# Two layers of a hybrid trunk: the down projection as plain sums over all channel tiles in place of a Strassen form

## The chip, the cores and the metric

The kernel runs on one core of one Trainium2 chip. The metric is the device time of one execution in microseconds (us).

## The reference

Two layers work on 1024 latent and 128 context tokens of 1024 channels, in float32. Each layer has a mixer (retention, Fourier mixing, latent attention, long convolution) and then a channel sub-layer. The change lies in the end of the channel sub-layer, the product with `w_down`, and in what comes right after it:

```
h = rmsnorm(x, norm[2]) * (1.0 + sc2) + sh2
f = (jax.nn.silu(h @ p['w_gate']) * (h @ p['w_up'])) @ p['w_down']
x = x + g2 * rmsnorm(f, norm[3])
```

`w_down` is 2816 x 1024 per layer. The next layer begins with `rmsnorm(x, norm[0]) * (1.0 + sc1) + sh1` and the input projection.

## The kernel before

The 1152 tokens are nine tiles of 128 (tile 8 is the context, `CTX`), the 2816 hidden channels are 22 tiles (`NF`). A float32 product is made of three products of split operands: `split` (L119 to L125) writes a rounded high part on ACT (L120) and the remainder on DVE (L125), and `mm3` (L127 to L131) issues three matmuls, high by high, high by low and low by high, each with 128 hidden channels and 128 tokens as the stationary operand and 512 columns moving. PSUM holds a 128x512 float32 block in a bank.

`channels(l)` runs `phase3` and `gate_up`, which writes the hidden rows tile by tile to DRAM (`self.hd`), and then `ffn(l)` (L1469 to L1705):

- The down projection is Winograd's form of Strassen's product over pairs of token tiles (0,1), (2,3), (4,5), (6,7), halves of a chunk of hidden channels and halves of the 1024 columns. `DOWN` names four chunks. For each chunk and pair, seven products (`product`, L1599) take the place of eight; tile 8 goes alone with four products.
- `load_w`, `sums_w` and `prep_w` (L1494 to L1514) load a chunk's weights (tile `b`), add and subtract their blocks on POOL and DVE (`bt`) and split them into `dw`. `load_h` and `prep_h` (L1525, L1534) load hidden rows (`hraw`, `h`), form block sums (`hx`) and split them into the ring `ho`.
- A product of `dw` and `ho` fills one PSUM bank `dq`; its result is added on ACT, DVE and POOL (`ups`, `acc`) into sums in SBUF, one tile `acc` of 128x1024 for each token tile.
- `chain(t)` (L1563) closes a token tile: mean square (ACT), reciprocal root (`rsqrt`, small DVE steps), times the gate's row (DVE), residual add (POOL or DVE, by `ET`), the store, and in layer 0 the next layer's norm (`norm_mod`). The transpositions of the nine tiles into `Th`, `Tl` (`norm_turn`, 72 of them) follow after all products, in layer 0 alone.

The order on each engine is set by a scheduler from the order of the code, shifted by `self.first(n)`; the list `groups` and the constants `AH`, `S_AT` set what is prepared how far ahead. Each engine then takes its instructions in order.

After layer 0's stage comes layer 1's `phase1`: the input projection (matmuls `acc<-whi,Th` of 288 columns), and the spectrum of a filter (`psf`, `g`, `gc`, `gabs`, `gsum`, then the transform at L224).

Of the kernel before, what the change touches and what calls it, by code (L numbers as in the profile page):

```python
# [10 lines left out]
F32 = mybir.dt.float32  # L11
F32R = mybir.dt.float32r
# [7 lines left out]
P = 128  # L20
L = 2
# [14 lines left out]
# ---------------------------------------------------------------- constants of the shapes  # L36
def shape_constants():
# [33 lines left out]
    # channel and position DFTs of the Fourier mixer  # L71
# [10 lines left out]
    # rotary tables, [token of the tile, tile, (first half, second half)]  # L82
# [8 lines left out]
    # retention: distances, masks (with the key scale), positions  # L91
# [7 lines left out]
# ---------------------------------------------------------------- kernel  # L99
class Kern:  # L100
# [12 lines left out]
    # -- small helpers  # L113
# [19 lines left out]
    def rsqrt(self, y, v, pool, tag):  # L133
        """y = v ** -0.5, [p, n]"""
# [20 lines left out]
    # -- two engines for plain arithmetic  # L155
# [13 lines left out]
    # ------------------------------------------------------------ hyena: filters  # L169
    # slots of a tile spectrum (value = re - i * im)  # L170
# [3 lines left out]
    def dft_odd(self, z, d, s, y, tmp):  # L174
        """odd classes from z0, z4 ([p, 1, c]), d, s ([p, 3, c])"""
# [42 lines left out]
    def fft_class(self, r, y, ps, cons, inverse):  # L218
        """ps [p, 2, c]: (re, im) of class r; cons [p, 3, 128]: cos, sin, -sin"""
# [88 lines left out]
    def norm_mod(self, t, x, y, ra, rb, psp, tag, r=None, e="g"):  # L308
        """tile t of the modulated norm of x, transposed and split into T"""
# [36 lines left out]
    def filter_mlp(self, h1p, h2p, psp, tag):  # L346
        """hidden rows of the filter networks of both layers (64 rows each), to DRAM; the second copy runs backwards"""
# [27 lines left out]
    def filter_spectrum(self, l, o, p1, p2, psp, tag):  # L375
        """spectrum of filter o of layer l, to DRAM"""
# [44 lines left out]
        # the direct term: the filter at distance 0, before the division by the norm  # L421
# [46 lines left out]
    def long_conv(self, l, o, z, gate, p1, p2, psp, tag):  # L468
        """z = gate * conv(z), [p, 9, 256] (tile 8: context); the direct term is part of the filter"""
# [43 lines left out]
        # the parts of the way to the spectrum, and of the way back, in time for the classes that need them  # L513
# [91 lines left out]
    def hu_block(self, l, b, wp, h1p, sp, psp, ztile, xg):  # L605
        """128 channels of the hyena input: projection, short convolution, back to token rows"""
# [9 lines left out]
        # tokens 0..1023 at 1.., the context's at 1027.., zeros around both  # L616
# [32 lines left out]
    def phase1(self, l):  # L649
        nc, tc, A = self.nc, self.tc, self.A  # L650
        with ExitStack() as c:
# [7 lines left out]
            if l == 0:  # L659
# [8 lines left out]
                # shift and scale of one half of the columns, then of the other  # L668
# [21 lines left out]
                with tc.high_priority(offset=0):  # L690
                    for q in (0, 2, 1, 3):
# [10 lines left out]
                        # the row of the samples and that of the context, to all partitions  # L702
# [164 lines left out]
    def head_load(self, l, h, pool, hd, psp):  # L867
        """transposed and split q, k (zeros below the 96 features), the split v of head h"""
# [21 lines left out]
    def att_scores(self, t, ops, pool, psp):  # L890
        """exp(scores - max) of query tile t and 1 / (its row sums)"""
# [33 lines left out]
    def att_out(self, l, h, tiles, pT, rs, vhl, pool, psp):  # L925
        """probabilities times v, over the row sums"""
# [939 lines left out]
```

## Time and profile before

| | |
|---|---|
| three runs, us | 3521.51, 3522.32, 3538.58 (median 3522.32) |
| span of the profiled execution | 3531.2 us; its own device time is not listed |
| PE busy | 3206.7 us (91%) in 18934 matmuls |
| DVE busy | 2700.7 us (76%) |
| ACT, POOL busy | 1286.5 us (36%), 1122.7 us (32%) |
| HBM read, written | 303.03 MB, 92.00 MB: 112 GB/s over the span |
| down projection, `dq` matmuls | 2112 in two stages, 1532.2 to 1841.9 us and 3229.0 to 3513.4 us |

Busy time counts an instruction from start to end. Matmuls overlap in the array, so the distance between two starts says how fast they go, and the busy time says less. A wait is put down to the event that came last before an instruction could start. The granted clock of PE is given as a share of full speed.

### The profile page before, as it was taken

What the parts mean: (1) busy time and instruction counts of PE and PEld (TensorE: products, weight loads), DVE (VectorE), ACT (ScalarE), POOL (GpSimd) and SP (SyncE); (2) the same over time, 40 slices, a digit from 0 to 9 for tenths busy, and PEclk for the clock granted to TensorE, in tenths of its full rate; (3) what the DMA queues carried; (4) which work ended last, traced back from release to release, by engine and by line L of the source; (5) the groups of instructions that cost most, each with busy time, mean ns of one, the idle gap of its engine ahead of it and who ended that gap; (6) DMA issues with size and microseconds to landing.
All of it is one profiled execution on the core that took longest, in us unless ns stands there. A gap on an engine that the chain in (4) does not pass through costs nothing.

```text
span 3531.2 us, 52713 instructions
## 1 busy us (share of the span) xinstructions
PE 3206.7 (91%) x18934; PEld 2830.7 (80%) x18934; DVE 2700.7 (76%) x5024; ACT 1286.5 (36%) x2496; POOL 1122.7 (32%) x947
## 2 busy tenths in 40 slices
PE   8899888999879999989968998899996999999897
PEld 5768777888779999967747787798885999998775
DVE  6676796767898888898897627666788866668898
ACT  3123113545444444443323232254544322223332
POOL 2111430001255555546661014201012422223664
PEclk8899899889989999999987999998898999999998
DMA  5454455104333344343223534531143322213223
GB/s 209 131 168 131 142 157 181 50 17 149 117 111 118 117 129 119 96 134 113 91 88 126 158 108 132 181 106 34 33 165 108 104 74 74 74 58 110 96 72 135
DMA packets 323349, 398.50 MB, mean 113 GB/s; under 512 B 60266, under 2 KB 253543, under 8 KB 322576
## 3 DMA queue, kind: packets, MB, share of 16 engines
q1 hardware_dynamic: 261312, 338.16, 30.1%
q10 hardware_dynamic: 61776, 56.97, 5.2%
q8 instruction: 150, 2.46, 0.3%
q14 instruction: 111, 0.91, 0.1%
HBM read 303.03 MB, written 92.00 MB: 112 GB/s over the span
## 4 chain that ended last, share of the span: by engine, by line
PE 55%; DVE 23%; DMA 6%; issue 6%; POOL 5%; ACT 4%; SPq 0%; ACTq 0%; DVEq 0%; POOLq 0%
PE gu L129 8%; PE gu L131 8%; PE gu L130 8%; DVE ho L125 3%; PE acc L131 3%; PE acc L130 2%; PE acc L129 2%; DMA adw<-in_wada 2%; DVE rq_w L146 2%; DVE acc L157 1%; DVE dw L125 1%; PE pstr L917 1%; DVE adacc L160 1%; POOL acc L157 1%; PE psr L1109 1%
## 5 line engine op out<-in xcount | busy, mean ns | idle before, releaser
L129 PE MATMUL dq<-dw,ho 128*128 128x512 f32 x704 | 289.3, 412 | 47.0 <-DVE acc L157 17.9
L131 PE MATMUL dq<-dw,ho 128*128 128x512 f32 x704 | 289.2, 411 | 34.9 <-DVE ho L125 34.7
L129 PE MATMUL gu<-X,fw 128*128 128x256 f32 x1024 | 290.1, 286 | 7.9 <-ACT fw L120 4.4
L160 DVE SCALAR_TENSOR_TENSOR adacc<-adw,csilu,adacc 128x256 f32<-128x256 f32 x392 | 239.7, 638 | 71.1 <-DMA adw<-in_wada 70.2
L131 PE MATMUL gu<-X,fw 128*128 128x256 f32 x1024 | 287.1, 283 | 1.8 <-DVE fw L125 1.8
L130 PE MATMUL dq<-dw,ho 128*128 128x512 f32 x704 | 287.1, 408 | 0.3 <-DVE dw L125 0.2
L130 PE MATMUL gu<-X,fw 128*128 128x256 f32 x1024 | 285.9, 282 | 0.0
L130 PE MATMUL acc<-wlo,Th 128*128 128x256 f32 (+1 forms) x720 | 217.4, 303 | 5.6 <-DVE wlo L125 5.6
L129 PE MATMUL acc<-whi,Th 128*128 128x256 f32 (+1 forms) x720 | 219.4, 307 | 0.0
L131 PE MATMUL acc<-whi,Tl 128*128 128x256 f32 (+1 forms) x720 | 215.8, 301 | 0.0
L129 PEld LDWEIGHTS dq<-dw,ho 128*128 128x128 f32 x704 | 138.2, 196 | 88.1 <-issue 41.6
L129 PEld LDWEIGHTS gu<-X,fw 128*128 128x128 f32 x1024 | 193.1, 190 | 18.6 <-ACT fw L120 8.1
L131 PEld LDWEIGHTS dq<-dw,ho 128*128 128x128 f32 x704 | 138.1, 196 | 78.3 <-DVE ho L125 45.4
L157 POOL TENSOR_TENSOR adacc<-adacc,adp 128x256 f32<-128x256 f32 x168 | 153.7, 915 | 131.4 <-ACT adp L272 124.4
L131 PEld LDWEIGHTS gu<-X,fw 128*128 128x128 f32 x1024 | 193.3, 190 | 2.3 <-DVE fw L125 2.3
L130 PEld LDWEIGHTS gu<-X,fw 128*128 128x128 f32 x1024 | 193.7, 190 | 0.0
L120 ACT ACTIVATE ho<-hraw 128x384 fp32r<-128x384 f32 (+1 forms) x192 | 87.8, 489 | 272.4 <-POOL hraw L157 254.7
L129 PE MATMUL gu<-x1s,fw 128*128 128x320 f32 x576 | 178.8, 310 | 3.6 <-DVE u L157 3.1
L131 PE MATMUL gu<-x1s,fw 128*128 128x320 f32 x576 | 179.5, 312 | 2.1 <-DVE fw L125 2.0
L130 PE MATMUL gu<-x1s,fw 128*128 128x320 f32 x576 | 179.0, 311 | 0.0
L125 DVE TENSOR_TENSOR ho<-hraw,ho 128x384 fp32r<-128x384 f32 (+1 forms) x192 | 165.6, 879 | 8.1 <-ACT ho L120 8.0
L130 PEld LDWEIGHTS dq<-dw,ho 128*128 128x128 f32 x704 | 138.3, 196 | 32.9 <-DVE dw L125 1.2
(526 smaller groups left out, 10186.7 us busy)
## 6 DMA issues: line engine op xcount, KB each, us to landing
adw<-in_wada SPq DMA_DIRECT2D x320, 128.0 KB
h<-U SPq DMA_DIRECT2D x176, 128.0 KB
X<-in_wf SPq DMA_DIRECT2D x42, 512.0 KB
fr<-in_wf SPq DMA_DIRECT2D x40, 512.0 KB
b<-in_wf SPq DMA_DIRECT2D x24, 768.0 KB
hraw<-h SPq DMA_DIRECT2D x24, 768.0 KB
pj<-pst ACTq DMA_DIRECT2D x90, 128.0 KB
G<-gt SPq DMA_DIRECT2D x36, 256.0 KB
```

The source lines that it names most:

```text
L120: nc.scalar.activation(hi, src, AF.Copy)
L125: (nc.vector if elo == "dve" else nc.gpsimd).tensor_tensor(out=lo, in0=src, in1=hi, op=ALU.subtract)
L129: mm(ps, lh, rh, start=start, stop=False)
L130: mm(ps, lh, rl, start=False, stop=False)
L131: mm(ps, ll, rh, start=False, stop=stop)
L146: nc.vector.scalar_tensor_tensor(out=w, in0=a, scalar=a[:, 0:1], in1=v, op0=ALU.mult, op1=ALU.mult)
L157: (self.nc.vector if e == "v" else self.nc.gpsimd).tensor_tensor(out=out, in0=a, in1=b, op=op)
L160: self.nc.vector.scalar_tensor_tensor(out=out, in0=a, scalar=s, in1=b, op0=op0, op1=op1)
L917: T(pst[:, j], pr[i][:, (k0 + j) * P:(k0 + j + 1) * P], self.ident)
L1109: nc.tensor.matmul(pi[:, pr], qx[q, pr, d], Sall[q, t, pr, d], start=False, stop=d == 1)
```

## The change

`ffn` is written anew (L1462 to L1560) and the layout of the hidden rows in DRAM is one tensor of 128x9x128 for each channel tile. The Strassen form, its sums of operands and its sums of results in SBUF are gone. Three groups of three token tiles each run over all 22 channel tiles; each token tile's sum stays in two PSUM banks (`q0`, `q1`, `q2`, six banks) from the first channel tile to the last. One step (`prepare`) loads the weights of a channel tile (512 KB) and the hidden rows of it for the three token tiles of the group (192 KB), and splits both: 66 steps and 1188 matmuls in a layer, where there were 1056. The weights are so loaded three times. The channel tiles are taken in `BLOCKS` of three (the last of four), one token tile after the other. `finish(t, ps)` follows as a token tile's sum ends: it reads the sum from PSUM, stores the residual row, and in layer 0 it norms and transposes the tile at once.

```diff
-    DOWN = (0, 2), (4, 3), (10, 3), (16, 3)
-    RING, HRING, AH = 8, 7, 5
-    ET, LC, TP = (7, 1), (3, 3), (0, 100)
+    BLOCKS = (0, 3), (3, 3), (6, 3), (9, 3), (12, 3), (15, 3), (18, 4)
+    RING, AH = 6, 3
+    ET = (7, 1)
...
-            dn = Banks(c, tc, "dn", {"tr": 2, **{f"q{t}": 1 for t in range(6)}})
+            dn = Banks(c, tc, "dn", {"tr": 2, **{f"q{t}": 1 for t in range(3)}})
...
+            wh = [pool(f"wh{i}") for i in range(self.RING)]
+            hr = pool("hr", 4, side="right")
+            wr = pool("wraw", 3, side="right")
+            steps = [(g, f) for g in range(3) for f in range(NF)]
+            early = ("Th0", "Tl0", "Th1", "Tl1", "Th2", "Tl2")
+            def prepare():
+                s = len(W)
+                g, f = steps[s]
+                w = wr.tile([P, 8, P], F32, name="dwr")
+                nc.sync.dma_start(w, A["wf"][l, f, :, 16:24])
+                h = hr.tile([P, 3, P], F32, name="dhr")
+                nc.sync.dma_start(h, self.hd[l][f][:, 3 * g:3 * g + 3])
+                p, k = (self.tp, {"tag": early[s]}) if s < len(early) else (wh[s % self.RING], {})
+                t = p.tile([P, 2816], F32R, name="dw", **k)
+                cut = [t[:, a:b] for a, b in ((0, 1024), (1024, 2048), (2048, 2432), (2432, 2816))]
+                self.split(cut[2], cut[3], h.rearrange("p a b -> p (a b)"))
+                self.split(cut[0], cut[1], w.rearrange("p a b -> p (a b)"))
+                W.append(cut)
...
+            def finish(t, ps):
+                if t == CTX:
+                    load_rows(t)
+                x = fin.pop(t)
+                y = xp.tile([P, D], F32, name="y4", tag=f"y4{t % 2}")
+                r = self.rstd(y, ps, D)
+                e = "v" if t > self.ET[l] else "g"
+                cut = [slice(512 * h, 512 * h + 512) for h in range(2)] if last and t > 6 else [slice(0, D)]
+                for q in cut:
+                    self.stt(y[:, q], ps[:, q], r[:, 0:1], rows[0][:, q], ALU.mult, ALU.mult)
+                    self.tt(e, x[:, q], x[:, q], y[:, q], ALU.add)
+                    nc.sync.dma_start(self.xd[l + 1][t][:, q], x[:, q])
+                if not last:
...
+                    self.norm_mod(t, x, y, rows[1], rows[2], dn, "tr", None, e)
+                if t + 3 < NT:
+                    load_x(t + 3)
...
+            for g in range(3):
+                ps = [dn.tile([P, D], F32, name="dq", tag=f"q{j}") for j in range(3)]
+                for f0, n in self.BLOCKS:
+                    for j in range(3):
+                        want = min(NF * g + f0 + n + (j + 1) * self.AH // 3, len(steps))
+                        while len(W) < want:
+                            prepare()
+                        for f in range(f0, f0 + n):
+                            wh_, wl_, hh, hl = W[NF * g + f]
+                            q = slice(j * P, j * P + P)
+                            for hs in (slice(0, 512), slice(512, 1024)):
+                                self.mm3(ps[j][:, hs], hh[:, q], hl[:, q], wh_[:, hs], wl_[:, hs], f == 0, f == NF - 1)
+                        if f0 + n == NF:
+                            finish(3 * g + j, ps[j])
```

How the instructions then stand is shown at three places. The first is PE in layer 0 where the first group of token tiles ends: `dq_16239` is the sum of tile 2, `dq_16971` that of tile 3, `y4_16753` the normed tile 0.

```order
L129 MATMUL dq_16239<-dw_16715 128x512
L130 MATMUL dq_16239<-dw_16715 128x512
L324 MATMUL pstr_16789<-ident_66,y4_16753 128x128 x4
L324 MATMUL pstr_16796<-ident_66,y4_16753 128x128 x4
L131 MATMUL dq_16239<-dw_16715 128x512
L129 MATMUL dq_16971<-dw_16724 128x512
```

Tile 0's eight transpositions stand ahead of the last matmul of its group. Tile 1's stand 52 matmuls later and tile 2's 94 later, and the second group ends in the same way.

The second place is ACT behind that group's end. `y4_16838` and `dq_16238` belong to tile 1, `y4_16921` and `dq_16239` to tile 2, `x4_16545` is tile 1's residual row; L302 is the sum of squares.

```order
L120 ACTIVATE Th0_16771<-pstr_16789 128x4x128
L120 ACTIVATE Th0_16771<-pstr_16796 128x4x128
L120 ACTIVATE dw_17032<-dhr_17030 128x384
L120 ACTIVATE dw_17032<-dwr_17028 128x1024
L302 ACTIVATE y4_16838,ss_16856<-x4_16545 128x1024
L302 ACTIVATE y4_16921,ss_16922<-dq_16239 128x1024
L120 ACTIVATE Th0_16771<-pstr_16872 128x4x128
```

The sum of squares of tile 2's sum stands behind that of tile 1's residual row, which exists only when tile 1's sum has been read, scaled and added. On DVE the read of tile 1's sum (`y4_16838<-dq_16238`) stands behind the splits of tile 0's transpositions and of the steps before `dw_17032`'s weights.

The third place is PE behind layer 0's last `dq`. Before:

```order
L131 MATMUL dq_18506<-dw_17737,ho_18431 128x512
L391 MATMUL psf_18843<-w3_18837,hc_18839 128x256 x2
L391 MATMUL psf_18851<-w3_18837,hc_18847 128x256
L324 MATMUL pstr_18623<-ident_66,acc3_16245 128x128 x4
L391 MATMUL psf_18851<-w3_18837,hc_18847 128x256
L324 MATMUL pstr_18630<-ident_66,acc3_16245 128x128 x4
```

Now:

```order
L324 MATMUL pstr_18285<-ident_66,y4_18242 128x128 x4
L130 MATMUL dq_17722<-dw_18213 128x512
L131 MATMUL dq_17722<-dw_18213 128x512
L129 MATMUL acc_18986<-whi_18964,Th0_16771 128x288
L129 MATMUL acc_19015<-whi_18964,Th0_16771 128x288
L129 MATMUL acc_19044<-whi_18964,Th0_16771 128x288
```

The next layer's input projection on tiles 0 to 2 stands directly behind the last `dq`. The transpositions of tile 7 stand 42 projection matmuls further on, those of tile 8 another 45 or so, and the filter's first transform (L224) stands behind 330 projection matmuls, where it stood behind 261.

## Rows read from the trace of the kernel before

**Rows 1.** Windows: length, busy (count) PE, PEld, DVE, ACT, POOL, clock, DMA share, GB/s

```profile
1532.20:1841.90 309.70, 269.16 (x1060) 205.47 (x1060) 286.08 (x385) 107.26 (x196) 192.56 (x127) 0.93 0.29 102
1841.90:1893.40 51.50, 34.20 (x104) 22.73 (x105) 44.83 (x103) 17.80 (x36) 14.08 (x6) 0.54 0.48 155
1893.40:1942.10 48.70, 44.37 (x274) 40.49 (x272) 37.56 (x42) 14.53 (x34) 6.76 (x6) 0.92 0.31 98
...
3229.00:3513.40 284.40, 259.61 (x1056) 204.32 (x1056) 259.92 (x334) 100.47 (x185) 168.51 (x116) 0.96 0.30 102
3513.40:3531.20 17.80, 0.00 (x1) 0.00 (x0) 13.74 (x40) 2.89 (x10) 0.00 (x0) 0.55 0.32 118
1640.00:1660.00 20.00, 20.00 (x87) 16.18 (x87) 17.84 (x16) 9.26 (x11) 14.19 (x10) 1.00 0.14 44
3441.00:3464.00 23.00, 23.00 (x101) 18.55 (x99) 19.58 (x37) 6.17 (x16) 15.27 (x12) 1.00 0.51 183
```

**Rows 2.** Timeline, PE, a full-clock stretch: start, length, instruction

```profile
1640.07 0.40 PE L129 MATMUL dq<-dw,ho 128*128 128x512 f32 x1
1640.30 0.40 PE L130 MATMUL dq<-dw,ho 128*128 128x512 f32 x1
```

**Rows 3.** Waits of PE, layer 0 stage: us in total, times, longest

```profile
PE dq L131 <- DVE ho L125: 21.7, 11, 5.7
PE dq L129 <- DVE G L157: 9.5, 1, 9.5
PE dq L129 <- DVE acc L157: 8.1, 5, 3.6
```

**Rows 4.** Waits of PE, layer 1 stage

```profile
PE dq L131 <- DVE ho L125: 13.0, 5, 4.1
PE dq L129 <- DVE acc L157: 9.8, 6, 3.6
```

**Rows 5.** Timeline, PE, behind a wait in the layer 0 stage

```profile
1629.67 0.63 PE L130 MATMUL dq<-dw,ho 128*128 128x512 f32 x1
...
1632.65 0.63 PE L131 MATMUL dq<-dw,ho 128*128 128x512 f32 x1
```

**Rows 6.** Groups by shape, layer 0 stage: busy, mean ns, idle before

```profile
L125 DVE TENSOR_TENSOR ho<-hraw,ho 128x384 fp32r<-128x384 f32 x72 | 67.1, 949 | 2.6 <-ACT ho L120 2.6
...
L157 POOL TENSOR_TENSOR x<-x,acc 128x1024 f32<-128x1024 f32 x6 | 14.6, 2436 | 7.4 <-issue 3.2 <-DVE ss L303 1.8 <-DVE rs L153 1.3
...
L302 ACT ACTIVATE acc<-x 128x1024 f32<-128x1024 f32 x6 | 6.4, 1059 | 24.0 <-POOL x L157 24.0
```

**Rows 7.** Line L125 on DVE: ns min/median/max of one

```profile
L125 DVE TENSOR_TENSOR ho<-hx,ho x32: 404/548/1409, 1538.2 to 3495.0; 128x384 fp32r<-128x384 f32 x24, 128x256 fp32r<-128x256 f32 x8
...
L125 DVE TENSOR_TENSOR mixs<-mix,mixs x18: 1207/1218/1226, 844.3 to 2674.3; 128x1024 fp32r<-128x1024 f32 x18
```

**Rows 8.** Line L120 on ACT: ns min/median/max of one

```profile
L120 ACT ACTIVATE mixs<-mix x18: 1042/1046/1061, 842.5 to 2670.7; 128x1024 fp32r<-128x1024 f32 x18
```

**Rows 9.** DMA view, 3221 to 3229 us, 40 slices of 0.2 us

```profile
GB/s 236 328 358 410 369 420 389 430 410 482 369 430 410 471 307 184 0 0 0 0 0 0 0 0 0 0 0 0 143 164 82 123 215 307 389 399 410 399 420 399
```

**Rows 10.** Timeline, the end of layer 1

```profile
3516.00 1.28 DVE L160 SCALAR_TENSOR_TENSOR acc<-acc,rs,r 128x1024 f32<-128x1024 f32 x1
...
3521.66 0.60 ACT L1568 ACTIVATE sq<-acc 128x512 f32<-128x512 f32 x1 [6.06 <-DVE acc L157]
...
3523.47 0.15 DVE L160 SCALAR_TENSOR_TENSOR ss<-ss 128x1 f32<-128x1 f32 x1
...
3525.38 1.42 DVE L160 SCALAR_TENSOR_TENSOR acc<-acc,rs,r4c 128x512 f32<-128x512 f32 x2
```

**Rows 11.** Timeline, DVE, behind the layer 0 stage

```profile
1901.70 0.68 DVE L400 TENSOR_TENSOR gc<-psf,wn 128x512 f32<-128x512 f32 x1
```

**Rows 12.** Timeline, PE, behind the layer 0 stage

```profile
1891.83 1.94 PE L324 MATMUL pstr<-ident,acc 128*128 128x128 f32 x8 [1.78 <-DVE acc L157]
...
1942.07 0.70 PE L224 MATMUL psf<-gy,hcons 128*128 128x256 f32 x2 [0.20 <-DVE gy L157]
```

More of the change, by code (lines that the diff above doesn't have):

```diff
@@ L1421, in product @@
                         self.stt(U, U, 0.5, G, ALU.mult, ALU.mult)
-                        k = max(k for k in range(len(self.DOWN)) if self.DOWN[k][0] <= f)
-                        for v in (0, 1, 2)[:2 + ch]:
-                            hd = self.hd[l][k][2 * ch + v][:, f - self.DOWN[k][0]]
-                            nc.sync.dma_start(hd.rearrange("p (a c) -> p a c", a=2), U[:, :, P * v:P * v + (P if v < 2 else 64)])
+                        hd = self.hd[l][f]
+                        for a in range(2):
+                            nc.sync.dma_start(hd[:, 4 * ch + a:4 * ch + a + 3:2], U[:, a, 0:2 * P].rearrange("p (v c) -> p v c", v=2))
+                        if ch:
+                            nc.sync.dma_start(hd[:, 8].rearrange("p (a c) -> p a c", a=2), U[:, :, 2 * P:2 * P + 64])
             todo = [(u, i) for u in range(len(units)) for i in range(7)]
@@ L1471, in ffn @@
         last = l == L - 1
[L1472 to L1474 removed]
+        with ExitStack() as c:
+            dn = Banks(c, tc, "dn", {"tr": 2, **{f"q{t}": 1 for t in range(3)}})
             pool = lambda nm, bufs=1, **k: c.enter_context(tc.tile_pool(name=nm, bufs=bufs, reuse_waits="tile", **k))
[L1476 to L1587 removed]
@@ new lines, in ffn @@
+            wh = [pool(f"wh{i}") for i in range(self.RING)]
+            rp = pool("r4")
+            xp = pool("x4")
+            hr = pool("hr", 4, side="right")
+            wr = pool("wraw", 3, side="right")
+            steps = [(g, f) for g in range(3) for f in range(NF)]
+            early = ("Th0", "Tl0", "Th1", "Tl1", "Th2", "Tl2")
+            W = []
+            def prepare():
[11 more added lines that the diff above has]
+                W.append(cut)
@@ L1589, in load_x @@
+            rows, fin = {}, {}
             def load_x(t):
@@ L1646, in step @@
-            def step(g):
-                if next(g[1], 0) == 0:
-                    chains.remove(g)
-                    if g[0] + 3 < NT:
-                        load_x(g[0] + 3)
-            groups, hops = [], []
-            for u, (k, v) in enumerate(units):
-                if k < NC - 1 and v == 3:
-                    groups += [(u, 0), (u + 1, 0), (u, 1), (u, 2), (u + 1, 1), (u, 3), (u, 4), (u + 1, 2), (u, 5),
-                               (u + 1, 3), (u, 6)]
-                    hops += [(u, 0), (u + 1, 0), (u, 1), (u, 2), (u, 3), (u, 4), (u + 1, 2), (u, 5), (u + 1, 1), (u, 6)]
-                elif v < 4:
-                    groups += [(u, j) for j in range(7)]
-                    hops += [(u, j) for j in range(7)]
-                elif k == NC - 1:
-                    groups += [(u, j) for j in range(4)]
-                    hops += [(u, i) for i in (0, 2, 1)]
@@ L1665, in ffn @@
-            reads = lambda u, j: (u, (0, 0, 2, 1)[j] if units[u][1] == 4 else j)
-            lastread = {reads(*g): i for i, g in enumerate(groups)}
-            W_AT = (4, 0), (3, 1), (4, 1), (3, 3), (4, 2), (4, 3)
-            ops, chains = [], []
-            with self.first(1500):
-                load_w(0)
-                load_h(0)
-                load_h(1)
-            with self.first(0):
-                for i in range(7):
-                    prep_w(0, i)
-                    for j in range(0 if i else 3):
-                        sums_w(0, j)
-                    if i == 5:
-                        sums_w(0, 3)
-                    prep_h(0, i) if i < 6 else None
@@ L1727, in ffn, with load_rows @@
-            while chains:
-                for g in list(chains):
-                    step(g)
+                fin[t] = x
+            def load_rows(t):
+                for i, (m, s) in enumerate(((l, 5),) if last else ((l, 5), (l + 1, 1), (l + 1, 0))):
+                    rows[i] = rp.tile([P, D], F32, name=f"r4{i}")
+                    self.row(rows[i], m, s, t)
+            def finish(t, ps):
[11 more added lines that the diff above has]
+                if not last:
+                    if t % 3 == 0:
+                        for nm in "hl":
+                            getattr(self, f"T{nm}")[t // 3] = self.tp.tile([P, 8, 384], F32R, name=f"T{nm}{t // 3}")
+                    self.norm_mod(t, x, y, rows[1], rows[2], dn, "tr", None, e)
+                if t + 3 < NT:
+                    load_x(t + 3)
@@ L1730, in ffn @@
             if not last:
                 self.Th, self.Tl = [None] * 3, [None] * 3
-                for g in (1, 0, 2):
-                    self.Th[g] = self.tp.tile([P, 8, 384], F32R, name=f"Th{g}")
-                    self.Tl[g] = self.tp.tile([P, 8, 384], F32R, name=f"Tl{g}")
-                    for t in range(3 * g, 3 * g + 3):
-                        self.norm_turn(t, acc[t], dn, "tr")
+            with self.first(1500):
+                for _ in range(3):
+                    prepare()
@@ new lines, in ffn @@
+            with self.first(600):
+                for _ in range(3):
+                    prepare()
+            for g in range(3):
[4 more added lines that the diff above has]
+                        while len(W) < want:
+                            prepare()
+                        for f in range(f0, f0 + n):
[5 more added lines that the diff above has]
+                            finish(3 * g + j, ps[j])
+                    if g == 0 and f0 == 9:
+                        load_rows(0)
+                        for t in range(3):
+                            load_x(t)
@@ L1750, in run @@
                   for l in range(L) for o in range(2) for r in (*range(9), "c")}
-        self.hd = [[[self.dram([P, 2 * n, 256 if v < 4 else P], f"h{l}_{k}_{v}") for v in range(5)]
-                    for k, (_, n) in enumerate(self.DOWN)] for l in range(L)]
+        self.hd = [[self.dram([P, NT, P], f"h{l}_{f}") for f in range(NF)] for l in range(L)]
         self.qd, self.kvd, self.krd = {}, {}, {}
```

200 lines of the change are left out of this document (removed).

## The prediction

> **What bounds the kernel now.** I read the table of windows first, since only the two stages of `dq` matmuls and what follows each can change. From layer 0's first `dq` to the next layer's first filter transform 309.7 + 51.5 + 48.7 = 409.9 us pass; from layer 1's first `dq` to the end 284.4 + 17.8 = 302.2 us [rows 1]. PE shows 269.16 us of 309.7 as busy, but a matmul that is shown as 0.40 us long is followed by the next after 0.23 [rows 2], so busy time is not the need. In two stretches at full clock 87 matmuls go in 20.0 us and 101 in 23.0 [rows 1]: 0.230 and 0.228 us each. At 0.230 the 1056 matmuls of a stage need 242.9 us. Layer 0's stage is 66.8 us longer than that, layer 1's 41.5. The waits say why: PE stands for splits of hidden operands (`ho`, 21.7 and 13.0 us) and for banks that DVE has not yet emptied (`acc`, 8.1 and 9.8) [rows 3, 4]. Behind a wait matmuls go at half clock: eight of them begin in the 2.98 us from 1629.67 to 1632.65, 0.426 from start to start [rows 5]. DVE, which PE waits for, is itself busy 286.08 of 309.7 us, beside a POOL that is busy 192.56 [rows 1]; its 128x384 split of `hraw` takes 949 ns on average there, where the median of a like one is 548 [rows 6, 7].
>
> **What the change removes and adds in the stages.** Every sum of operands and of results goes, and nearly all POOL work with them. A layer gets 132 more matmuls: 132 x 0.230 = 30.4 us, all on PE and hidden by nothing. In return the waits may go, if a step's preparation is short. A step has 18 matmuls, 4.14 us. Its preparation costs DVE 0.55 + 1.22 = 1.77 us [rows 7]; on ACT 1.05 us for the weights [rows 8] and, as an estimate by the same ratio of columns, 0.4 to 0.5 for the hidden rows: 1.5 us. Both engines are under half loaded, without POOL beside them. The loads are 704 KB (0.72 MB) in 4.14 us, 174 GB/s, all issued on SP. The stage moved 102 GB/s before, but one stretch moved 183 at a DMA share of 0.51 [rows 1], and slices with transfers of 768 KB in flight show 389 to 430 [rows 9]. So I cost the loads at nothing: they lie beside the matmuls, with about a block of three channel tiles (12.4 us) of lead. Without that cover they would set the pace; that is the first rival.
>
> Each stage's start costs the wait for the last gate (9.5 us, layer 0 [rows 3]) as now. The splits of the first steps stand on DVE and ACT among the last gate's work: +2 us a layer, bounds -2 and +8.
>
> **The ends of the groups.** This is what layer 0 pays. Call the end of a group's first sum 0. ACT's sum of squares takes 1.06 us and its read-out 0.2 or so [rows 6], the small root steps 3523.47 to 3525.38, 1.9, and the scaling 1.28 [rows 10]: 4.7 with latencies. The residual add on POOL takes 2.44 [rows 6]: 7.3. The second sum of squares ends at 8.6. Tile 1's first one, in line behind it on ACT, ends at 9.9, and DVE works both roots together: the norm's scaling ends at 13.3 and POOL's add at 15.8. The transpositions stand ahead of the group's last matmul, which PE reaches at 48 x 0.23 = 11: a wait of 5 us. In the next group the fourth tile finds its bank free (since 4.7). The fifth needs tile 1's bank, whose read stands behind the splits of tile 0's transpositions and of two steps on DVE: about 21.9 against 21.4, 0.5 us. The sixth needs tile 2's: its sum of squares stands on ACT behind tile 1's second one, so tile 1's scaling (21.9), POOL's add (24.4), two sums of squares (27.0), the root (29) and scaling come first: 30.5 against 26.2, 4.3 us. That is 10 us a boundary, and 3 more for two runs of matmuls at 0.43 instead of 0.23 [rows 5]. Two boundaries: 26 us. Bounds: 5 each if the scheduler's overlaps are kinder, 20 each if DVE and POOL again slow each other as `ho` shows (949 against 548). I take 13, since the chain's durations are already those beside a busy neighbour. In layer 1 there is no norm and no transposition: a bank is free 4.7 us after its sum ends, and is wanted 11 later. I allow 3 us (0 to 8).
>
> The transpositions of tiles 0 to 6, 56, now lie in the stage. Eight take 1.94 us [rows 12] in a stretch whose clock is 0.54 [rows 1]; at full clock I take half, 0.12 each: 6.8 us (up to 13.6).
>
> **The tails.** Layer 0's end was 51.5 + 48.7 = 100.2 us from the last `dq` to L224. Now projection on tiles 0 to 2 starts at once. The same chain as above gives tile 7's transpositions at 26 (counted from the end of tile 6's sum), where PE arrives at 23, and tile 8's at 36.5, then nine filter products between some 45 projection matmuls of 0.16 us (44.37 us for 274 instructions [rows 1]): the filter's last row `gc` at about 48. From `gc` to L224 the trace shows 1942.07 - 1901.70 = 40.4 us [rows 11, 12], on ACT and DVE, and no part of that changes. So L224 stands at 88.4, or 77 after the nominal last `dq` (88.4 - 11.4, as tile 6's sum ends that much earlier). If PE alone decided it would be 330 x 0.16 + 5 + 8 = 67; with a slower chain 88. By then 69 more projection matmuls are done than before, 11 us of PE; PE waits some 10 us for L224 either way, so I credit 5 (0 to 11). Layer 1's end shrinks: from the sum of squares at 3521.66 to the span's end at 3531.2 are 9.5 us [rows 10], and now that is nearly all that is behind the last matmul: 10 instead of 17.8.
>
> **The sum.** Layer 0: 1188 x 0.230 = 273.2, + 6.8 + 26 + 2 + 77 = 385.0 against 409.9, and the credit of 5: 30 us saved. Layer 1: 273.2 + 2 + 3 + 10 = 288.2 against 302.2: 14 saved. Together 44. The profiled span, 3531.2, is 8.9 above the median of the runs; I take the difference from the median: 3522.3 - 44 = **3478 us**.
>
> **Rivals.**
> - **Loads set the pace, slower.** 66 x 0.72 = 47.6 MB a layer come through one queue, with rows of 4 KB and 1.5 KB, and SP's queue also holds stores that wait for the tails. For it: the stage never moved more than 183 GB/s over 23 us [rows 1]. Against it: the slices of 400 [rows 9]. The gain of 44 is gone when both stages together take 44 us longer, near 315 us a layer or 151 GB/s, since layer 0's 35 us of waits and transpositions would hide part of it. At 140 a layer takes 340 us; layer 1's stage (278 by the sum) grows by 62 and layer 0's (308) by 32: 94 - 44 = 50 slower, 3572. The Trainium skill (DMA: Bandwidth & Descriptors, "Anatomy of one DMA — SWDGE (gpsimd) path") fits about 2.0 us plus bytes over 436 GB/s for one DMA of another kind of issue; taken one after the other that would be 5.7 us a step and about 3640 in all.
> - **The tails eat it, no change.** Each of the two boundaries and the tail costs some 15 us more than I worked out, because ACT and DVE take each tile's chain in order with the steps of the next group behind it. For it: small root steps and splits that take double beside POOL [rows 6, 7]. Price: about 3520.
> - **A quicker pace, faster.** Half the half-clock distance of 0.426 [rows 5] is 0.213: at full clock the array itself needs that for 512 columns, and 17 ns of the 230 are something else. If they come from what the plain form lacks (results read from six banks, sums beside them), 2376 x 0.017 = 40 us more go: 3438. Against it: the two stretches that wait for nothing differ in what lies beside them (POOL busy 14.19 of 20.0 and 15.27 of 23.0 us, 44 and 183 GB/s) and agree to 2 ns [rows 1]. The Trainium skill (TensorE: Matmul & The Clock Gate, "Wait — 56ns, not 53.3ns?") gives 215.7 ns from start to start for 512 columns when warm; the trace does not agree, at 230, and by the page the sum would be 34 us lower, 3444.
>
> **How the numbers follow.** Forecast 0.70, with a range of its own of 3448 to 3508 (boundaries 5 to 20, tail 67 to 88, starts and credit by their bounds, not all at one end). Loads 0.09, tails 0.17, pace 0.04. A measurement of this kernel tells 0.5%, 17.6 us, from no change: faster means below 3504.7. The forecast, the quicker pace and a sliver of the tails give faster 0.77; the rest of the tails 0.13 the same; loads and the worst tails 0.10 slower. The range is 3442 to 3515.
>
> **What would show it.** Right: stages of about 308 and 278 us with clock near 0.98 in layer 1, `dq` starts 0.230 apart inside groups, no wait of `dq` for `dw` in mid-group, POOL nearly idle, waits of 3 to 6 us at transpositions and at the third tile of a group in layer 0 alone, and about 10 us behind layer 1's last matmul. Wrong: repeated waits for `dw` that end on `dwr` or `dhr` loads (first rival), boundaries of over 20 us or L224 later than 88 us (second), starts nearer 216 ns (third).

## The result, and the profile after

| kernel | us, median of its runs | ratio to the kernel before, 95% interval |
|---|---|---|
| before | 3523.98 (3521.51 to 3538.58) | |
| changed | 3483.86 (3473.26 to 3492.61, 4 runs) | 0.9864 [0.984, 0.9889] |
| changed, once more | 3481.06 (3476.07 to 3493.07, 4 runs) | 0.9871 [0.9842, 0.9899] |

The change saves 40 us by the medians, 1.1% to 1.6% by the interval. (The medians alone give a ratio of 0.9886; the ratios of the table are those on record, and the second one was taken beside other runs of the kernel before, with a median of 3528.03.) The profiled execution of the changed kernel was its quickest run, 3473.26 us with a span of 3471.5.

The windows of the changed kernel, with the same columns as those of before: layer 0's stage, from its last `dq` to the filter's transform, layer 1's stage, its end.

```profile
1528.10:1838.20 310.10, 287.47 (x1245) 235.66 (x1245) 156.67 (x288) 109.43 (x168) 38.42 (x14) 0.96 0.53 171
1838.20:1914.40 76.20, 70.43 (x395) 62.07 (x395) 59.66 (x88) 23.89 (x51) 10.42 (x8) 0.91 0.45 140
3187.20:3462.10 274.90, 272.79 (x1188) 224.65 (x1188) 130.38 (x211) 93.32 (x139) 5.71 (x2) 0.99 0.54 179
3462.10:3471.50 9.40, 0.00 (x0) 0.00 (x0) 4.50 (x14) 1.10 (x2) 0.00 (x0) 0.70 0.52 167
```

Against [rows 1]: layer 0's stage is as long as it was (309.7) with 132 matmuls more in it; layer 1's is 9.5 us shorter. DVE is busy 156.67 and 130.38 us where it was 286.08 and 259.92, POOL 38.42 and 5.71 where it was 192.56 and 168.51. The end of layer 0 takes 76.2 us in place of 100.2, that of layer 1 9.4 in place of 17.8. Transfers, stores included, run at 171 and 179 GB/s.

The waits of PE in the two stages, against [rows 3, 4] (us in total, times, longest), layer 0 first:

```profile
PE pstr L324 <- POOL y L157: 22.5, 7, 4.5
PE dq L129 <- ACT dw L120: 0.7, 1, 0.7
```

```profile
PE dq L129 <- ACT dw L120: 12.3, 1, 12.3
PE dq L129 <- DVE y L160: 2.1, 2, 1.8
```

All waits for operands and for sums in mid-stage are gone. What is left in layer 0 stands at the transpositions, seven times, and is of POOL's last add (`y`). The 12.3 us in layer 1 is the start of the stage. The timeline of PE at the first group's end shows three of the seven:

```profile
1625.27 1.97 PE L324 MATMUL pstr<-ident,y 128*128 128x128 f32 x8 [4.54 <-POOL y L157]
...
1642.84 1.70 PE L324 MATMUL pstr<-ident,y 128*128 128x128 f32 x8 [2.41 <-POOL y L157]
...
1657.63 1.09 PE L324 MATMUL pstr<-ident,y 128*128 128x128 f32 x8 [2.51 <-POOL y L157]
```

By place, in us from the profiles (the second profile of the changed kernel, of a run of 3493.07, in the last column):

| from, to | before | changed | again |
|---|---|---|---|
| layer 0: last gate matmul to L224 | 419.7 | 401.1 | 401.1 |
| L224 to layer 1's first gate matmul | 776.7 | 764.6 | 771.9 |
| layer 1's gate_up | 502.3 | 495.6 | 497.0 |
| layer 1: last gate matmul to the end | 310.1 | 296.9 | 295.0 |
| sum of these | 2008.8 | 1958.2 | 1965.0 |

So 18.6 us come from layer 0's stage and end, 13 to 15 from layer 1's, 5 to 12 from the mixer between them, which starts with 69 more projection matmuls done, and 5 to 7 from layer 1's gate_up, whose code the change does not touch. The mixer's share is not clear of the differences between executions: it took 759 to 772 us in the twelve profiles of the changed kernel and its variants, 776.7 in that of the kernel before, and 802.9 in a variant of the latter (the first experiment) that leaves the mixer as it was. Up to layer 0's last gate matmul the code is the same; the executions differ by some 10 us there.

### The profile page after: what moved, and what is told of

Read it like the earlier page. It is cut to its first block, busy times and chain, and to the rows that moved or that the text cites. A ratio compares the mean times of both kernels' runs of the same rounds, so it can differ in the third digit from the quotient of the medians.

```text
span 3471.5 us, 52716 instructions
## 1 busy us (share of the span) xinstructions
PE 3193.9 (92%) x19198; PEld 2840.6 (82%) x19198; DVE 2408.6 (69%) x4726; ACT 1271.5 (37%) x2384; POOL 776.5 (22%) x705
## 4 chain that ended last, share of the span: by engine, by line
PE 40%; DVE 8%; DMA 3%; issue 2%; POOL 2%; ACT 2%; SPq 0%; DVEq 0%; ACTq 0%; POOLq 0%
PE dq L129 4%; PE dq L130 4%; PE dq L131 4%; PE gu L129 4%; PE gu L131 4%; PE gu L130 4%; PE acc L131 1%; PE acc L130 1%; PE acc L129 1%; PE pstr L917 1%; DMA wn<-in_win 1%; DVE rq_w L146 1%; PE psr L1109 1%; DMA adw<-in_wada 1%; POOL y L157 1%
## 5 line engine op out<-in xcount | busy, mean ns | idle before, releaser
L129 PE MATMUL dq<-dw 128*128 128x512 f32 x792 | 313.1, 395 | 15.2 <-ACT dw L120 13.0
L130 PE MATMUL dq<-dw 128*128 128x512 f32 x792 | 312.5, 395 | 0.0
L131 PE MATMUL dq<-dw 128*128 128x512 f32 x792 | 311.3, 394 | 0.0
L125 DVE TENSOR_TENSOR dw<-dhr,dw 128x384 fp32r<-128x384 f32 x132 | 74.6, 570 | 213.6 <-ACT dw L120 213.6
L129 PEld LDWEIGHTS dq<-dw 128*128 128x128 f32 x792 | 151.2, 191 | 49.1 <-ACT dw L120 14.2
L125 DVE TENSOR_TENSOR dw<-dwr,dw 128x1024 fp32r<-128x1024 f32 x132 | 161.5, 1226 | 29.2 <-ACT dw L120 28.9
L131 PEld LDWEIGHTS dq<-dw 128*128 128x128 f32 x792 | 151.0, 191 | 32.2 <-DVE dw L125 0.5
L130 PEld LDWEIGHTS dq<-dw 128*128 128x128 f32 x792 | 151.5, 191 | 31.3
```

The lines of the kernel that those rows point to most:

```text
L125: (nc.vector if elo == "dve" else nc.gpsimd).tensor_tensor(out=lo, in0=src, in1=hi, op=ALU.subtract)
L129: mm(ps, lh, rh, start=start, stop=False)
L130: mm(ps, lh, rl, start=False, stop=False)
L131: mm(ps, ll, rh, start=False, stop=stop)
```

## Experiments

**Where the Strassen form's waits came from.** The sums of results with an earlier chunk's block are left out of the kernel before:

```diff
                     if k:
-                        self.tt("v" if k == NC - 1 and v >= self.LC[l] else "g", o, o, b, ALU.add)
                         b = o
...
-                    if k:
-                        self.tt(self.EC, c11, c11, p1, ALU.add)
```

> The kernel before, with the sums of results that add an earlier chunk's block left out (POOL's adds of ups into acc, and the last chunk's ones on DVE): a part of the result is missing. Theory (PE waits in the Strassen form because DVE is slowed and held up by POOL's work and the sums): the stages fall from 309.7 and 284.4 by 25 to 45 and 15 to 30 us, DVE's 128x384 split falls from 949 toward 700 ns, and waits of dq for acc go. Rival (PE waits for the hidden operands' own chain from load over sum to split, whatever else runs): the stages fall by under 10 each and the wait for ho stays at about 20 and 13.

Two runs, 3471.58 and 3497.95 us; ratio 0.9876 [0.981, 0.9942]. Its stages:

```profile
1534.00:1811.20 277.20, 261.49 (x1060) 205.37 (x1060) 256.50 (x380) 108.29 (x195) 125.60 (x82) 0.94 0.33 112
...
3225.00:3478.80 253.80, 250.27 (x1056) 200.96 (x1056) 233.65 (x339) 103.18 (x190) 100.15 (x71) 0.98 0.34 115
```

They are 32.5 and 30.6 us shorter, as the theory had it, and PE's wait for `ho` falls from 21.7 to 10.3 us in layer 0 and from 13.0 to 3.5 in layer 1. (The time falls by less than these 63 us: in this profile, of the run of 3497.95 us, the mixer took 26 us more than in that of the kernel before.) DVE's 128x384 split takes 755 ns where it took 949 [rows 6]:

```profile
L125 DVE TENSOR_TENSOR ho<-hraw,ho 128x384 fp32r<-128x384 f32 x72 | 53.2, 755 | 6.6 <-ACT ho L120 6.6
```

A second cause is not separated from this one. POOL also makes sums of hidden operands (`hraw`, `hx`), in line with the sums that were left out, and ACT rounds such an operand only behind its sum. ACT's wait for them falls too, in layer 0 from the first line to the second:

```profile
ACT ho L120 <- POOL hraw L157: 112.8, 30, 10.6
ACT ho L120 <- POOL hraw L157: 77.9, 26, 7.4
```

So PE may wait less because DVE splits faster, because POOL's own line is shorter, or for both reasons. The next run tests the first by itself, in a form without such a line.

The same from the other side: the plain form, with POOL work that nothing needs. This builds on the run with the tails' adds on DVE (below), in which POOL is idle in the stages.

```diff
+                self.tt("g", scr[1], w.rearrange("p a b -> p (a b)"), scr[0], ALU.add)
                 W.append(cut)
```

> The kernel of the run with all tail adds on DVE, and in each step one 128x1024 add on POOL more, of the raw weights into a scratch tile that nothing reads: POOL is busy for about 2.4 us in 4.1, near its share in the Strassen stages (192.56 of 309.7 us). Theory (POOL's work beside DVE's splits is what filled DVE in the Strassen form): the 128x384 split goes from 551 ns to 750 to 950 on average, the 128x1024 one from 1.22 us to 1.6 to 2.0, DVE's busy time in layer 1's stage from 131 to 175 to 220 us; PE waits little, since DVE still has room: layer 1's stage 273 to 280. Rival (DVE is slowed in the Strassen form by its own order and waits, not by POOL): the splits stay within 10% of their times.

One run, 3543.23 us, against 3445.82 without that add. DVE's two splits in layer 1's stage, with POOL's work and then without:

```profile
L125 DVE TENSOR_TENSOR dw<-dwr,dw 128x1024 fp32r<-128x1024 f32 x58 | 90.6, 1563 | 4.0 <-ACT dw L120 4.0
L125 DVE TENSOR_TENSOR dw<-dhr,dw 128x384 fp32r<-128x384 f32 x66 | 55.1, 844 | 90.8 <-ACT dw L120 90.6
```

```profile
L125 DVE TENSOR_TENSOR dw<-dwr,dw 128x1024 fp32r<-128x1024 f32 x58 | 70.7, 1220 | 10.4 <-ACT dw L120 10.4
L125 DVE TENSOR_TENSOR dw<-dhr,dw 128x384 fp32r<-128x384 f32 x66 | 36.3, 553 | 114.4 <-ACT dw L120 114.3
```

The 128x384 split slows by half on average (its median is 548 ns with and 551 without that work, but some splits take up to 2758), and DVE's busy time in that stage goes from 131 to 198 us, as expected. That PE would wait little was wrong: the stages grew from 280.4 and 273.5 to 333.2 and 303.1 us.

```profile
1536.40:1869.60 333.20, 291.12 (x1237) 237.54 (x1236) 235.73 (x299) 108.39 (x165) 145.69 (x58) 0.93 0.50 161
...
3229.00:3532.10 303.10, 278.14 (x1188) 226.47 (x1188) 197.89 (x214) 92.54 (x138) 143.05 (x57) 0.95 0.49 163
```

DVE has room on average, but not at the groups' ends, where tails and splits stand in one line: its reads of `dq` and its small root steps are what PE waits for there (20.0 us in layer 1 for `y`). The add also holds a load's buffer longer, so not all of the growth is DVE's. The Trainium skill (SBUF — State Buffer, "Who interferes with whom") states that a DVE instruction with two inputs in SBUF contends with a GpSimd instruction that reads SBUF; both splits are of that kind, and 844 against 553 ns agrees.

**Are the loads near a limit?** Each step's weights are loaded a second time.

```diff
+                w2 = wx.tile([P, 8, P], F32, name="dwx")
+                nc.sync.dma_start(w2, A["wf"][l, f, :, 16:24])
```

> The changed kernel with each step's weights loaded a second time into a buffer that nothing reads: 1.25 MB a step, 300 GB/s at full pace. Theory (loads lie beside the matmuls with a large reserve): the stages grow by under 15 us each, no wait of dq for dw in mid-group, time within 3484 to 3510. Rival (the single queue was near its limit, the prediction's first rival): the stages grow by 60 us or more each, dq waits for dw and dw for dwr.

3476.43 us (3470.06 to 3484.47), no slower. The two stages move 276 and 304 GB/s:

```profile
1532.10:1846.50 314.40, 290.33 (x1249) 237.04 (x1250) 171.21 (x294) 114.57 (x172) 41.60 (x19) 0.96 0.77 276
...
3183.50:3459.00 275.50, 272.75 (x1188) 224.23 (x1188) 135.53 (x215) 99.17 (x140) 5.70 (x2) 0.99 0.82 304
```

The first rival of the prediction falls: at 179 GB/s the queue is far from its limit.

**What the order of the tails is worth.** First the transpositions of tiles 0 to 5 are moved to the third, fourth and fifth block of the next group:

```diff
-                    self.norm_mod(t, x, y, rows[1], rows[2], dn, "tr", None, e)
+                    self.norm_mod(t, x, y, rows[1], rows[2], None, None, None, e)
+                    pend.append((t, y))
...
+                        if pend and f0 in (6, 9, 12) and j == 0:
+                            turn()
```

> The changed kernel with one part altered: the transpositions of tiles 0 to 5 in layer 0 are issued 108 or more matmuls into the next group in place of 1, 52 and 94. Theory (order of the tail: PE stands at the transpositions for POOL's last add, 22.5 us in seven waits, all else is free): six of the seven waits and the half-clock matmuls behind them go, layer 0's stage falls from 310 to 288 (285 to 292) us and the time by about 20 to 3464. Rival (banks: behind the transposition waits stand waits for the banks of the group's second and third tile, as the prediction's sum had them, 4.8 us a boundary): the stage falls by 12 at most, and dq waits for DVE's read of dq at the two boundaries. Rival (loads are late behind the tails): waits of dq for dw appear after the boundaries.

3472.03 us (3467.15 to 3478.25), ratio 0.984 [0.9798, 0.9881]; layer 0's stage 303.8 us. The waits of PE in it:

```profile
PE dq L129 <- DVE y L160: 10.6, 4, 3.2
PE pstr L324 <- POOL y L157: 3.6, 1, 3.6
PE dq L130 <- DVE dw L125: 3.5, 2, 1.8
```

The first rival held. The transpositions' waits went, and behind them stood what the prediction's sum had at this place: waits for the banks of the group's second and third tile (10.6 us at two boundaries), and a short one for a split.

Then only tiles 0 to 2 are turned within the stage, and tiles 3 to 8 behind the last `dq`:

```diff
+            while pend:
+                turn()
```

> The changed kernel with the transpositions of tiles 3 to 8 in layer 0 issued only behind the last dq, as the kernel before did with all nine; tiles 0 to 2 as in the run before this one. Theory (the gain at layer 0's end, 100 to 76 us from the last dq to the filter's transform, comes from tails that follow as each sum ends): the stage loses its waits (about 285 us), but the end grows from 76 to 90 to 100 us; the time is at or above that of the changed kernel, 3475 to 3495. Rival (the end is set by the filter's chain on DVE and ACT alone, and the order of the tails is worth little): the end stays near 76 and the time falls to about 3462.

3473.68 us (3463.1 to 3475.74).

```profile
1532.50:1824.80 292.30, 278.16 (x1215) 227.84 (x1215) 151.88 (x276) 103.39 (x158) 40.70 (x13) 0.99 0.55 177
1824.80:1913.80 89.00, 77.58 (x440) 69.69 (x438) 67.40 (x103) 29.25 (x60) 12.39 (x9) 0.88 0.44 136
```

The end grows to 89 us, as the theory had it, but the stage shortens by as much: 381.3 us for both, against 379.3 in the run before and 386.3 in the changed kernel. For tiles 3 to 5, following each sum with its transpositions is worth nothing by itself; it moves waits from the end into the stage. Tiles 0 to 2 were turned within the stage in every run, so that part is not tested. The time is a little below what the theory had (3475 to 3495).

**What makes the boundary long.** All adds of the tails go to DVE:

```diff
-    ET = (7, 1)
+    ET = (-1, -1)
```

> The changed kernel with all adds of the tails (residual, and in layer 0 the norm's shift) on DVE in place of POOL. Theory (the chain from a sum's end to its transpositions sets the boundary waits, and POOL's 2.4 to 3.3 us adds are 5 of its 16 us): PE's wait for transpositions in layer 0 falls from 22.5 to 6 to 12 us, layer 0's stage from 310 to about 297, the time by 10 to 14 to 3472. Rival (DVE, given the adds, splits later and PE waits for dw): the stage stays at 306 to 312.

3445.82 us (3438.05 to 3458.31), ratio 0.9764 [0.9739, 0.979]: 38 us below the changed kernel, three times what was expected.

```profile
1543.60:1824.00 280.40, 279.03 (x1237) 228.41 (x1236) 159.20 (x298) 107.87 (x166) 0.00 (x0) 0.99 0.58 189
1824.00:1902.00 78.00, 69.03 (x405) 62.80 (x405) 58.94 (x95) 25.38 (x53) 4.91 (x6) 0.93 0.43 137
```

```profile
PE pstr L324 <- DVE y L157: 1.2, 4, 0.4
```

The stage loses 29.7 us, and PE waits 1.2 us at transpositions instead of 22.5. Two things add up. The chain from a sum's end to its transpositions goes from 15.2 us (sum of squares at 1610.12, transpositions at 1625.27) to 12.9 (1625.16 to 1638.01). And with the shorter chain the scheduler places the transpositions of tiles 0, 1 and 2 at the 403rd, 461st and 523rd `dq` in place of the 395th, 448th and 490th, so that little is left to wait for; the half-clock stretches go as well, the stage's clock is 0.99 where it was 0.96. The shares of the two were not separated.

**The start of the stage.** It took 14.8 and 12.6 us from the last gate matmul to the first `dq`, where it had taken 9.8 and 7.9. In the changed kernel SP issues the first hidden rows among the stores of the last gate products, and ACT waits for them; this is layer 1:

```profile
3180.92 0.89 SPq L1424 DMA_DIRECT2D h<-U  x2
3181.86 1.95 SPq L1490 DMA_DIRECT2D dhr<-h  x4
```

```profile
3186.58 2.10 ACT L120 ACTIVATE dw<-dhr 128x384 fp32r<-128x384 f32 x4 [1.41 <-DMA dhr<-h]
```

```diff
-            hr = pool("hr", 4, side="right")
+            hr = pool("hr", 4)
+            pool("pad", side="right").tile([P, 1536], F32, name="pad")
```

> The changed kernel with the four buffers of hidden rows moved to another place in SBUF, one that gate_up gives free earlier; a pad of the same size stands where they were, so that nothing else moves. Theory (the start of the stage, 14.8 and 12.6 us from the last gate matmul to the first dq against 9.8 and 7.9 before, is the wait of the first hidden rows for a buffer that the last gate unit's tanh holds): the rows load before the last unit ends, the start falls to 2 to 5 us in both layers and the time by about 18 to 3466 (3460 to 3474). Rival (the start is set by the last unit's gate work on ACT and DVE and by the splits of six weight tiles in line with it): it stays above 9 us and the time moves by less than 5.

3471.62 us (3469.56 to 3473.91), ratio 0.9832 [0.9816, 0.9849]. The starts fell to 10.4 and 7.1 us, about what they were in the kernel before, and no further: the first `dq` now waits for DVE to read the last gate product out of its bank. In layer 0:

```profile
PE dq L129 <- DVE G L157: 10.2, 1, 10.2
```

So the place of the buffers cost some 5 us of each start, and the rest of the start is the gate work, as the rival said. In layer 1 most of it is won: from the last gate matmul to the end it is 290.2 us, against 296.9 and 295.0. In layer 0 nothing is won: four small products (`psada`) that had stood ahead of the first `dq`, where PE waited 11.8 us for their operand, now stand behind it, PE waits for them there, and the stage takes 314.7 us in place of 310.1; from the last gate matmul to L224 it is 402.1, against 401.1. The median time is 9 to 12 us below the two of the changed kernel, but its interval overlaps with theirs.

**All three together.**

> The changed kernel with three parts together: hidden rows in the place that comes free early, tail adds on DVE, transpositions of tiles 0 to 5 later. Theory (the parts add up, since they shorten different waits): starts of 2 to 5 us, layer 0's stage 285 to 292, time 3445 (3438 to 3455). Rival (what one part wins is lost behind it, in banks read late or in the filter's chain): 3458 or more.

3445.98 us (3428.35 to 3456.89), ratio 0.9757 [0.9724, 0.979]. The stages take 281.7 and 272.6 us. The time is what the theory named (3445), but not for its reason: the adds on DVE alone give 3445.82, so the parts do not add up. The starts, 9.5 and 6.7 us, missed the forecast of 2 to 5. In layer 0 the stage of the adds alone was 280.4, so with the short chain the later transpositions had nothing left to win; the rival's reason held, its time (3458 or more) did not. Both versions beat the kernel before and the changed one.

**Why matmuls start 227 ns apart and not 230.** In a full-clock stretch of the changed kernel 90 matmuls are counted in 20.0 us, where it was 87 [rows 1]. Such a count takes in matmuls that the stretch's start and end cut, so 20.0 divided by it is too short; the starts themselves are 226.8 ns apart here on average, and 232 in the two stretches of the kernel before.

```profile
3400.00:3420.00 20.00, 20.00 (x90) 16.57 (x89) 5.58 (x8) 5.64 (x9) 0.00 (x0) 1.00 0.55 178
```

It is not the work beside: with POOL's adds in every step the starts stay at 227, and in the Strassen form without POOL's sums they stay at 232. Two more runs, the first with the halves of the columns as the outer loop, the second with the split hidden rows in tiles of their own:

```diff
-                        for f in range(f0, f0 + n):
...
-                            for hs in (slice(0, 512), slice(512, 1024)):
+                        for hs in (slice(0, 512), slice(512, 1024)):
+                            for f in range(f0, f0 + n):
```

> The changed kernel with the two column halves as the outer loop of a block, so that 9 or 12 matmuls in a row add to one PSUM bank as in the Strassen form, where the changed kernel goes over to the other bank after every three. It asks why dq starts are 227 ns apart in it and were 232. Theory A (the change of bank): 232 again, layer 1's stage 275 to 281 us. Theory B (less work of DVE, ACT and POOL beside it): 227 stays.

One run, 3475.58 us, layer 1's stage 273.6: 227 stayed, theory A fell.

```diff
-                t = p.tile([P, 2816], F32R, name="dw", **k)
+                t = p.tile([P, 2048], F32R, name="dw", **k)
+                u = ho[s % 7].tile([P, 2, 3, P], F32R, name="ho")
```

> The changed kernel with the split hidden rows in a ring of tiles of their own, 128x768, where the changed kernel keeps them behind the weights in one tile of 128x2816. It asks again why dq starts are 227 ns apart and were 232 on average (stretches of 227 and longer ones of 232 and 235). Theory A (it is where the two operands of a matmul lie to each other in SBUF): starts spread over 227 to 235 again, layer 1's stage 278 to 282 us. Theory B (it is something else in the Strassen form): 227 stays, 273 to 276.

One run, 3490.58 us, layer 1's stage 274.5: 227 again, which by what was expected speaks against the addresses. But the addresses of the tiles in the built programs sort the starts, and in this kernel they leave both operands of most matmuls at the same offset. The last run moves the hidden rows' tiles of that kernel by 32 bytes (with them the residual rows behind them in SBUF, which no `dq` reads):

```diff
+            pool("shift").tile([P, 8], F32, name="shift")
             ho = [pool(f"ho{i}") for i in range(7)]
```

> The kernel of the run with the split hidden rows in tiles of their own, with those tiles moved by 32 bytes in SBUF. Read by address, the starts of the kernel before are 227 ns apart where weights and hidden rows both begin at a multiple of 128 bytes and 233 where the weights begin 96 bytes past one; in that run they are 227 with both 32 bytes past one and 229 with weights at 96 and rows at 32. Theory (the offset between the two operands modulo 128 bytes sets the pace): weights at 32 and rows at 64 give about 233, layer 1's stage 279 to 283 us against 274.5. Rival (the address of the weights alone, or something else of the Strassen form): 227 and 273 to 276.

One run, 3490.01 us. Layer 1's stage before the shift, and after it:

```profile
3204.90:3479.40 274.50, 272.18 (x1188) 223.92 (x1188) 129.16 (x212) 93.58 (x138) 4.98 (x2) 0.99 0.53 180
```

```profile
3197.30:3479.10 281.80, 280.43 (x1188) 224.75 (x1188) 129.41 (x212) 95.02 (x138) 4.98 (x2) 0.99 0.53 175
```

As many matmuls, waits within 2 us of each other, 7.3 us more; layer 0's stage goes from 318.3 to 326.8. The times of the two single runs do not show it, because up to layer 0's gates and in the mixer the second execution was quicker by some 18 us. Mean distance of the starts at full clock, by where the two operands begin (bytes past a multiple of 128):

| kernel | weights | hidden rows | starts | ns |
|---|---|---|---|---|
| before | 96 | 0 | 1500 | 233.3 |
| before | 0 | 0 | 397 | 228.1 |
| changed | 32 | 32 | 2121 | 226.8 |
| changed | 96 | 96 | 189 | 227.2 |
| rows apart | 32 | 32 | 2096 | 226.8 |
| rows apart | 96 | 32 | 196 | 229.1 |
| rows shifted | 32 | 64 | 2103 | 233.3 |
| rows shifted | 96 | 64 | 186 | 233.3 |

Operands that lie 32 or 96 bytes from each other modulo 128 cost 233; a distance of 0 gives 227 to 228 and one of 64 gives 229.

**The changed kernel once more.**

> The changed kernel once more, to place differences of some 10 us between the runs. Theory: a ratio to the kernel before within 0.984 to 0.989, a time of 3475 to 3492, layer 0's stage 310, layer 1's 275.

3481.06 us, ratio 0.9871 [0.9842, 0.9899], stages of 310.6 and 274.6.

## Why the prediction was right, and where its terms were off

The forecast was 3478 us, the runs give 3484 and 3481: a gain of 40 us, and of 47 against the runs beside the second, where 44 was worked out. The mechanism was the forecast one: the waits in mid-stage went, the pairs of stage and tail came out close to their sums, and the loads cost nothing. Term by term:

- **The waits of the Strassen form.** The prediction gave them to operands and sums that DVE, slowed by POOL, brings late. The run with POOL work beside the plain form shows that POOL's work slows DVE's splits and costs PE time; the one without POOL's sums shows that these sums cost the Strassen form some 30 us a stage, but not how much of it came by DVE and how much by POOL's own line of sums.
- **Matmuls.** 1188 x 0.230 = 273.2 us a stage was 3.5 too much: they go at 0.227. The 0.230 was itself misread, since it divides a stretch by a count that takes in cut matmuls: the starts in those two stretches are 0.232 apart. This is not the third rival's cause (results read from six banks, sums beside them), since a plain form with neither goes at 233 when its tiles are moved by 32 bytes; it is the addresses, and the rival's 213 ns never showed. The kernel before was at 232 on average, so 2376 x 0.005 = 12 us of the measured gain rest on where tiles happen to lie, and gate_up in layer 1, whose `fw` tiles also moved, gained 5 to 7 (seen in the traces, not tried by itself; layer 0's gate_up, whose tiles moved by as much, took 553.7 us against 551.6 and gained nothing).
- **The ends of the groups.** 10 us a boundary were worked out, and 9.5 measured (4.54 + 2.41 + 2.51). The first wait came as forecast, 15.2 us after the sum against 15.8. The other two were put down to banks and stood at transpositions; the bank waits lay hidden behind them and came out when the transpositions moved. Yet layer 0's stage as a whole was mis-sized: without its start the sum had 306 us, and it took 310.1 although its matmuls went 3.5 us quicker, so that 7 to 8 us more lie beside the matmuls. Of these 3.6 are a seventh wait, at tile 6's transpositions, that the sum did not have, and about one is the transpositions (0.14 us each, not 0.12); the rest is mostly matmuls at half clock, at the stage's start and behind the waits.
- **The starts.** +2 us a layer was mis-sized: +5.0 and +4.7. The prediction counted splits in line with the gate's work and not that the buffers of the hidden rows lie where the gate's tanh is written. That this is the cause is shown for layer 1; in layer 0 PE stood ahead of the first `dq` for the operand of `psada` as well.
- **Loads at nothing.** Right: 304 GB/s, 70% more than the 179 needed, went through without slowing the stage.
- **The tails.** Layer 0's end was forecast at 77 and took 76.2; layer 1's at 10 and took 9.4; the credit of 5 for the projection done ahead was 5 to 12 in two profiles, which is within what executions differ by there. For the end of layer 0 the length was right, but it is no gain of the new order by itself: with six tiles turned at the end, stage and end together were no longer.

The errors went both ways: 7 us of pace and 5 to 7 of gate_up for it, 6 us of starts and 7 to 8 of layer 0's stage against it. By place, layer 0's start, stage and end gave 18.6 us where 24.9 were worked out, and gate_up gave 5 to 7 that no term had. That the total came out within 4 us is in part luck. The second rival's price, 15 us more for each boundary, did not show here; work on POOL made for the test, beside the plain form, costs more than that.

## What to carry to other kernels

Before a form with fewer multiplications is kept, count what its sums do to the engines that feed the matmuls: here sums on POOL delayed the operands, in part by slowing DVE's splits, until the 132 matmuls saved per layer gave back no more than the waits cost. A tail that hangs on the end of a sum should run on the faster engine (an add of 128x1024 took 2.4 to 3.3 us on POOL and 1.2 on DVE): the two POOL adds in a chain of 15 us were worth 30 us in layer 0's stage and 38 in the median time, in part because the scheduler then placed the transpositions later. And a wait that is removed should be followed by a look at the one behind it.

## What was not expected of the hardware

The distance between the starts of these matmuls depends on the addresses of the two SBUF operands: 226.8 ns for 512 columns when weights and hidden rows begin at the same place modulo 128 bytes, 229.1 when they are 64 bytes off, 233.3 when they are 32 bytes off. The step from 226.8 to 233.3 was made by moving tiles, in one run, at the same granted clock of 0.99 over the stage, the same loads and the same work beside. In layer 1's gate_up of the changed kernel, whose weight tiles lie 96 bytes lower than before, the 256-column matmuls with these weights start 113.6 ns apart, with operands 64 bytes off, and 118.3 before, with operands 96 off. But the rule does not carry over to them as it stands: with the same addresses in layer 0 they start 116.4 ns apart (118.1 before), and some 300 with both operands at the same offset take 119 in both kernels. So something else acts there too, and it was not looked for. Why the distance matters was not tried, nor other offsets than multiples of 32 bytes. The Trainium skill (TensorE: Matmul & The Clock Gate, "Wait — 56ns, not 53.3ns?") has 215.7 ns for 512 columns; none of these runs comes nearer than 226.
